# A hybrid encoder block with a product-key expert layer: more expert tiles ahead, and new places for a gelu, casts, copies and loads in the gate stage

## The chip, the cores and the metric

The kernel runs on one core of one Trainium2 chip, as one program. Its time is the device time of an execution, in microseconds (us). The time before is the median of 3 runs, and one more execution was profiled: the page and the trace belong to that one. Engine names are those of the profile: PE is TensorE's matmuls and PEld its weight loads, DVE is VectorE, ACT is ScalarE, POOL is GpSimd, and SP is the queue that issues most transfers.

## The reference, cut to what matters

512 tokens of 1024 float32 values pass a mixing layer and then an expert layer (PEER). The mixing layer (a gated group and a banded attention group, about the first 225 us of the kernel) is not touched by the change. The expert layer is:

```python
def block(xb):                                   # 128 tokens at a time
    q = (xb @ w_query).reshape(128, 8, 2, 128)   # 8 heads
    sc = einsum('thpd,hpkd->thpk', q, sub_keys)  # two score lists of 128 keys
    s_top, i_top = lax.top_k(sc, 16)
    cand = s_top[:, :, 0, :, None] + s_top[:, :, 1, None, :]
    best, pos = lax.top_k(cand, 16)              # 16 experts of 16384 for each head
    g = softmax(best)
    h = gelu(einsum('thkd,td->thk', take(expert_u, eidx), xb))
    return einsum('thk,thkd->td', g * h, take(expert_v, eidx))
```

So each token meets 8 x 16 of 16384 experts, each with a row of 1024 values in `expert_u` and one in `expert_v`.

## The kernel before, in words

**Dense and gathered tokens.** The first 128 tokens have their expert rows gathered by indirect DMAs. The other 384 are computed densely, against all 16384 experts: a first product of the expert rows with the tokens (gelu of it is `act`), then `act` times a gate that is zero for experts not chosen, then a second product with the rows of `expert_v`. The last 64 of them are mixed: their first products are gathered (64 gathers of 128 rows, L655, with the dots on VectorE at L665), and only their second product is dense. Dense first products therefore have 320 tokens.

**Split operands.** Each float32 operand of a large matmul is split in two halves: ScalarE copies the upper part (`hi`, L155) and another engine subtracts to get the rest (`lo`, L156). That engine is VectorE or GpSimd, as the caller asks. Three matmuls (`mm3`, L194 to L196) make one k-step, and eight k-steps one tile of 128 experts. Two tiles are a chunk; there are 64 chunks. The tokens' own halves lie in `xbh`, `xbl`; from the gate stage on in `xch`, `xcl`, which GpSimd copies (L912, L913) in the loop over routed heads, both at head 4.

**Stages.** After the mixing layer, a loop over 8 heads (L884) does the queries, the scores, the top-16 searches on VectorE and some first products between them. The gate stage (L1011) builds the dense gate: for 8 tokens at a time GpSimd multiplies two digit patterns into `bm` (L964), VectorE builds a one-hot `am` (L972), and TensorE multiplies them (16 matmuls, L980); ScalarE copies the result out and stores it to DRAM. Its iterations run n = 0 to 49; `bm` of n is built in iteration n and multiplied in n + 2. The order of TensorE, VectorE, ScalarE and GpSimd is written out by hand there (`manual_schedule`), iteration by iteration: `bm`, products of n - 2, gelu of finished first products, `am`, one dot, one gather on GpSimd, then a share of first products (`multiply_some`, with `some` k-steps), then at most one split of a next tile (`split_next`). The splits that GpSimd takes here are all of those with n up to 5 and then every third tile.

**Early gate weights.** For the 64 mixed tokens, `weights_early` (L676) runs in two parts: at n = `own` - 7 = 33 a copy on VectorE and a DMA issued by GpSimd (L681, L682), at n = 35 a gelu on ScalarE in place and a product with the gates on VectorE (L684, L685). At n = 37 the gates of these tokens are transposed on TensorE (L942, L943).

**The second-product loop.** For chunks 0 to 63, `second_product` (L1143) multiplies `act` by the gate (L1153), splits it (L1154, L1155), and multiplies with rows of `expert_v` (36 matmuls of 512 columns, L1187); then first products of chunk c + AHEAD follow (`ahead`), as long as there are any. AHEAD is 23, so 46 tiles are made before the loop. Only TensorE's order is written out; the other engines' order comes from a planner with priorities, bounded by `queued_behind` and `issue_after`, which put instructions behind a named one on the same engine. Every third chunk from 0 routes one head of the gathered tokens (`route_gathered`, L1091: scores loaded, top-16 searches, `pairs` with two casts on ScalarE at L760 and L761, `choose`, softmax), and the gathers with their dots (L1111, L1113) and weighted sums (L1122, L1124) are spread over the chunks. Before the loop GpSimd's queue issues, in this order, the second part of the first gates (L997), two rows of tokens (L1087, L1089), and the scores of the first routed head (L1095).

## Time and profile before

| | us |
|---|---|
| median of 3 runs | 1427.35 (1424.94 to 1428.87) |
| the profiled execution | 1427.15 |
| its span, first to last instruction | 1425.1 |
| TensorE busy in it | 1390.5 |
| VectorE busy | 1152.2 |
| GpSimd busy | 705.3 |
| ScalarE busy | 614.3 |

In the profile, a row of a timeline gives the start, the length, the engine, the line of the code, the instruction with the tiles it writes and reads, how many are merged in the row, and in brackets the time the engine stood idle before it and what ended that. A row of the waits gives the engine and line that waited, what it waited for, the sum, the count and the longest. A row of busy times gives a stretch, its length, busy time and count for each of PE, PEld, DVE, ACT and POOL, then TensorE's granted clock (1.00 is full), the DMA engines' share and GB/s. Matmuls overlap, so a matmul's length in the trace is longer than the time from its start to the next one's; the text goes by starts.

### The profile page before, as it was taken

Reading aid. Unit: us, or ns where it says so; the run is one execution under the profiler, and the core shown is the slowest. Engines: PE = TensorE matmul, PEld = TensorE weight load, DVE = VectorE, ACT = ScalarE, POOL = GpSimd, SP = SyncE. Lnnn points to the kernel's source line nnn. Section 1 sums busy time; section 2 is a strip of 40 time slices with the busy share of each in tenths; the row PEclk is TensorE's granted clock in tenths of the full one; section 3 lists DMA queues with packets and bytes.
Section 4 is the critical chain, followed back from the end, with each engine's and each line's share of the span. In section 5 each row is a group of like instructions: output and inputs, shape, how many; then the busy total and the mean of one; then the engine's idle time right before and its main releaser. Section 6 shows DMA issues by size and latency. Waiting matters only on the chain.

```text
span 1425.1 us, 21665 instructions
## 1 busy us (share of the span) xinstructions
PE 1390.5 (98%) x7838; PEld 1229.4 (86%) x7838; DVE 1152.2 (81%) x2502; ACT 614.3 (43%) x957; POOL 705.3 (49%) x487
## 2 busy tenths in 40 slices
PE   9999999999998988999999999999999999999998
PEld 7887788898998887888998998998998988888887
DVE  5537745898997888699999999888978888688883
ACT  5447635443443444455444444343433333333331
POOL 0002104678789997344545656556545454254620
PEclk9999999999999999999999999999999999999999
DMA  4452225668677997968998999999999999689991
GB/s 164 132 192 74 104 75 192 208 223 278 226 246 245 331 339 221 334 239 318 341 349 335 361 340 368 338 376 372 379 334 358 350 341 376 236 328 350 343 335 70
DMA packets 164331, 396.24 MB, mean 278 GB/s; under 512 B 12881, under 2 KB 75233, under 8 KB 162177
## 3 DMA queue, kind: packets, MB, share of 16 engines
q1 hardware_dynamic: 64640, 194.14, 37.9%
q0 software_dynamic: 48176, 173.46, 33.2%
q10 hardware_dynamic: 51408, 27.27, 6.5%
q8 instruction: 61, 1.00, 0.3%
q14 instruction: 46, 0.37, 0.1%
HBM read 363.34 MB, written 31.46 MB: 277 GB/s over the span
## 4 chain that ended last, share of the span: by engine, by line
PE 56%; DVE 0%; issue 0%
PE pa L1187 24%; PE px L1187 12%; PE pu L194 7%; PE pu L195 7%; PE pu L196 7%; DVE res L1225 0%
## 5 line engine op out<-in xcount | busy, mean ns | idle before, releaser
L155 ACT ACTIVATE hi<-raw 128x1024 fp32r<-128x1024 f32 x296 | 313.0, 1059 | 477.2 <-DMA raw<-in_vd 129.0
L156 DVE TENSOR_TENSOR lo<-raw,hi 128x1024 fp32r<-128x1024 f32 x241 | 296.0, 1229 | 81.9 <-ACT hi L155 80.9
L1111 POOL DMA_INDIRECT row<-in_ud,eint x128 | 199.8, 1561 | 185.6 <-DVE acc L1124 129.3
L1122 POOL DMA_INDIRECT row<-in_vd,eint x128 | 184.2, 1439 | 173.1 <-DVE row L1113 118.8
L194 PE MATMUL pu<-xch,hi 128*128 128x320 f32 x784 | 248.3, 317 | 4.4 <-ACT act L718 4.4
L195 PE MATMUL pu<-xcl,hi 128*128 128x320 f32 x784 | 243.6, 311 | 0.0
L196 PE MATMUL pu<-xch,lo 128*128 128x320 f32 x784 | 243.5, 311 | 0.0
L1187 PE MATMUL pa<-lo,wh 128*128 128x512 f32 x512 | 199.8, 390 | 0.0
L1187 PE MATMUL pa<-hi,wh 128*128 128x512 f32 x512 | 199.3, 389 | 0.0
L156 POOL TENSOR_TENSOR lo<-raw,hi 128x1024 fp32r<-128x1024 f32 x55 | 131.2, 2400 | 117.6 <-ACT hi L155 116.8
L1124 DVE SCALAR_TENSOR_TENSOR acc<-row,hw,acc 128x1024 f32<-128x1024 f32 x128 | 164.6, 1286 | 2.0 <-DMA row<-in_vd,eint 1.8
L1187 PE MATMUL pa<-hi,wl 128*128 128x512 f32 x512 | 158.5, 389 | 0.0
L1113 DVE SCALAR_TENSOR_TENSOR row<-row,xb 128x1024 f32<-128x1024 f32 x128 | 157.2, 1231 | 0.1
L194 PEld LDWEIGHTS pu<-xch,hi 128*128 128x128 f32 x784 | 148.8, 190 | 6.6 <-ACT act L718 4.9
L195 PEld LDWEIGHTS pu<-xcl,hi 128*128 128x128 f32 x784 | 148.8, 190 | 1.6
L196 PEld LDWEIGHTS pu<-xch,lo 128*128 128x128 f32 x784 | 148.5, 189 | 0.0
L980 PE MATMUL pa<-bm,am 128*128 128x128 f32 x768 | 98.6, 283 | 16.8 <-POOL bm L964 16.2
L1187 PEld LDWEIGHTS pa<-hi,wh 128*128 128x128 f32 x512 | 96.1, 188 | 20.6
L1187 PEld LDWEIGHTS pa<-hi,wl 128*128 128x128 f32 x512 | 96.1, 188 | 20.3
L1187 PEld LDWEIGHTS pa<-lo,wh 128*128 128x128 f32 x512 | 96.1, 188 | 20.2
L980 PEld LDWEIGHTS pa<-bm,am 128*128 128x128 f32 x768 | 94.0, 198 | 20.5 <-POOL bm L964 19.3
L1187 PE MATMUL px<-hi,wh 128*128 128x512 f32 x256 | 100.2, 391 | 1.6 <-ACT hi L155 1.6
(236 smaller groups left out, 2635.5 us busy)
## 6 DMA issues: line engine op xcount, KB each, us to landing
raw<-in_uT SPq DMA_DIRECT2D x128, 512.0 KB
raw<-in_vd SPq DMA_DIRECT2D x128, 512.0 KB
gd<-gst ACTq DMA_DIRECT2D x24, 1024.0 KB
gc<-gd SPq DMA_DIRECT2D x15, 1280.0 KB
raw<-in_w_in SPq DMA_DIRECT2D x19, 512.0 KB
raw<-in_wq SPq DMA_DIRECT2D x16, 512.0 KB
raw<-in_w_out SPq DMA_DIRECT2D x8, 512.0 KB
gc<-gd SPq DMA_DIRECT2D x15, 256.0 KB
```

The costliest lines, as they stand in the source:

```text
L155: top = nc.scalar.activation(hi, raw, AF.Copy)
L156: ins = eng.tensor_tensor(lo, raw, hi.bitcast(F32), op=ALU.subtract)
L194: nc.tensor.matmul(ps, lh[0], rh[0], start=first, stop=False)
L195: nc.tensor.matmul(ps, lh[0], rh[1], start=False, stop=False)
L196: nc.tensor.matmul(ps, lh[1], rh[0], start=False, stop=last)
L980: nc.tensor.matmul(ps[:, i * P:(i + 1) * P], am[:, 4 * q + i, :], bm[:, 4 * q + i, :], start=True, stop=True)
L1111: nc.gpsimd.indirect_dma_start(out=row, out_offset=None, in_=ud, in_offset=bass.IndirectOffsetOnAxis(ap=eint[:, j:j + 1], axis=0))
L1113: nc.vector.scalar_tensor_tensor(row, row, 1.0, xb0, op0=ALU.mult, op1=ALU.mult, accum_out=hw[:, j:j + 1])
L1122: nc.gpsimd.indirect_dma_start(out=row, out_offset=None, in_=vd, in_offset=bass.IndirectOffsetOnAxis(ap=eint[:, j:j + 1], axis=0))
L1124: nc.vector.scalar_tensor_tensor(acc0, row, hw[:, j:j + 1], acc0, op0=ALU.mult, op1=ALU.add)
L1187: nc.tensor.matmul(accs[t][half], (wh, wh, wl)[k][:, b, tok], w[b][k % 2][:, ds_], start=first and k == 0, stop=last and k == 2)
```

## The change

Seven edits:

- AHEAD goes from 23 to 25: 50 tiles instead of 46 are made before the second-product loop, with two more `act` buffers; the scratch of GpSimd's DMA descriptors is halved (`SCRATCH`).
- In the gate stage a split goes to GpSimd only for every fourth tile, and from the first iterations on.
- `weights_early` has three parts: the copy at n = 33, the DMA at n = 34, gelu and product at n = 36. The gelu's result goes to PSUM, and the product reads it there.
- The casts of a routed head are queued behind the gelu last recorded (head 0) or the casts of the head before (later heads).
- The copies to `xch`, `xcl` are made in four pieces, one each at heads 1 to 4.
- The scores of routed head 0 are loaded first on GpSimd's queue, and the gates' second part and the two rows behind them.
- The gate products of chunk 0 are queued behind the last `am` of the gate stage.

```diff
-AHEAD = 23
+AHEAD = 25
...
-SCRATCH = 4096
+SCRATCH = 2048
...
             if part == 0:
                 nc.vector.tensor_copy(dots[own, :, 0, :], d[own])
+            elif part == 1:
                 nc.gpsimd.dma_start(dots[own, :, 1, :], d[0:P - UX])
             else:
-                nc.scalar.activation(dots[own], dots[own], AF.Gelu_apprx_tanh)
-                nc.vector.tensor_tensor(gate[own, TT - 1, :], gate[own, TT - 1, :],
-                                        dots[own].rearrange("p a b k -> p (a b k)"), op=ALU.mult)
+                ps = pa()[own, 0:NH * TOPK]
+                nc.scalar.activation(ps, dots[own].rearrange("p a b k -> p (a b k)"), AF.Gelu_apprx_tanh)
+                nc.vector.tensor_tensor(gate[own, TT - 1, :], gate[own, TT - 1, :], ps, op=ALU.mult)
...
-                nc.scalar.activation(first[:, 1], pos[:, :, 0, :], AF.Copy, scale=float(NK))
-                nc.scalar.copy(top[:, 1, :, 1, :], pos[:, :, 1, :])
+                with queued_behind(behind):
+                    casts = (nc.scalar.activation(first[:, 1], pos[:, :, 0, :], AF.Copy, scale=float(NK)),
+                             nc.scalar.copy(top[:, 1, :, 1, :], pos[:, :, 1, :]))
+                    routed[:] = [getattr(i, "ins", i) for i in casts]
...
-            if h == 4:
+            if 1 <= h < 5:
 
                 with queued_behind(splits):
-                    nc.gpsimd.tensor_copy(xch, xbh[:, :, T0:T0 + NDU])
-                    nc.gpsimd.tensor_copy(xcl, xbl[:, :, T0:T0 + NDU])
+                    ks = slice((h - 1) % 2 * KT // 2, ((h - 1) % 2 + 1) * KT // 2)
+                    to, of = ((xch, xbh), (xcl, xbl))[(h - 1) // 2]
+                    nc.gpsimd.tensor_copy(to[:, ks, :], of[:, ks, T0:T0 + NDU])
...
+            marked[:] = [getattr(ins, "ins", ins)]
...
-                if n == own - 5:
+                if n == own - 6:
                     weights_early(1)
+                if n == own - 4:
+                    weights_early(2)
...
-                    split_next(nc.vector if split % 3 and n > 5 else nc.gpsimd)
+                    split_next(nc.vector if split % 4 else nc.gpsimd)
...
+        def scores_of(b, eng):
             n = NH // PARTS
             sc = ep.tile([P, n, 2, NK], F32, name="sc0", tag="sc0", bufs=2)
-            (nc.sync if b else nc.gpsimd).dma_start(sc.rearrange("p h a n -> p h (a n)"), s0d[b * n:(b + 1) * n].rearrange("h p a -> p h a"))
+            load = eng.dma_start(sc.rearrange("p h a n -> p h (a n)"),
+                                 s0d[b * n:(b + 1) * n].rearrange("h p a -> p h a"))
+            return sc, getattr(load, "ins", load)
+
+        xb0 = ep.tile([P, D], F32, name="xb0")
+        acc0 = ep.tile([P, D], F32, name="acc0")
+        scores = {0: scores_of(0, nc.gpsimd)}
+        with tc.issue_after(scores[0][1]):
+            load_gates(0, nc.gpsimd, range(1, len(GROUPS)))
+            nc.gpsimd.dma_start(xb0, xbd[0])
+            nc.gpsimd.dma_start(acc0, x2d[0])
...
-            choose(ep, pairs(ep, top, pos, n), n, best, to, mask,
+            choose(ep, pairs(ep, top, pos, n, behind=list(routed if b else done)), n, best, to, mask,
```

More of the change, by code (lines that the diff above doesn't have):

```diff
@@ L681, in weights_early @@
                 nc.vector.tensor_copy(dots[own, :, 0, :], d[own])
+            elif part == 1:
                 nc.gpsimd.dma_start(dots[own, :, 1, :], d[0:P - UX])
             else:
-                nc.scalar.activation(dots[own], dots[own], AF.Gelu_apprx_tanh)
-                nc.vector.tensor_tensor(gate[own, TT - 1, :], gate[own, TT - 1, :],
-                                        dots[own].rearrange("p a b k -> p (a b k)"), op=ALU.mult)
-        begun, more, done, behind = [], [], [], []
+                ps = pa()[own, 0:NH * TOPK]
+                nc.scalar.activation(ps, dots[own].rearrange("p a b k -> p (a b k)"), AF.Gelu_apprx_tanh)
+                nc.vector.tensor_tensor(gate[own, TT - 1, :], gate[own, TT - 1, :], ps, op=ALU.mult)
+        begun, more, done, behind, routed = [], [], [], [], []
         open_tile = []
@@ L747, in best_keys, with pairs @@
             return top16(top[:, 0, u, p2, :], pos[:, u, p2, :], src, rep)
-        def pairs(pool, top, pos, n, ps=None, own=False):
+        def pairs(pool, top, pos, n, ps=None, own=False, behind=()):
             if ps is None:
@@ L971, in first_one_hot @@
             am = gp.tile(full, F32, name="am", tag="am", bufs=LEAD + 1)
-            nc.vector.tensor_tensor(am, iota_k[:, None, :].to_broadcast(full),
-                                    g[:, 0, c * TC:(c + 1) * TC, None].to_broadcast(full), op=ALU.is_equal)
+            ins = nc.vector.tensor_tensor(am, iota_k[:, None, :].to_broadcast(full),
+                                          g[:, 0, c * TC:(c + 1) * TC, None].to_broadcast(full), op=ALU.is_equal)
+            marked[:] = [getattr(ins, "ins", ins)]
             return am
@@ L988, in store @@
                                 st.rearrange("p (q b) t -> p q (b t)", b=GB))
-        gcs = {}
+        gcs, marked = {}, []
         def load_gates(q, eng, parts=range(len(GROUPS))):
@@ L1083, in hybrid_block @@
         gcp.append(ep)
-        load_gates(0, nc.gpsimd, range(1, len(GROUPS)))
+        def scores_of(b, eng):
+            n = NH // PARTS
+            sc = ep.tile([P, n, 2, NK], F32, name="sc0", tag="sc0", bufs=2)
+            load = eng.dma_start(sc.rearrange("p h a n -> p h (a n)"),
+                                 s0d[b * n:(b + 1) * n].rearrange("h p a -> p h a"))
+            return sc, getattr(load, "ins", load)
         xb0 = ep.tile([P, D], F32, name="xb0")
-        nc.gpsimd.dma_start(xb0, xbd[0])
         acc0 = ep.tile([P, D], F32, name="acc0")
-        nc.gpsimd.dma_start(acc0, x2d[0])
+        scores = {0: scores_of(0, nc.gpsimd)}
[3 more added lines that the diff above has]
+            nc.gpsimd.dma_start(acc0, x2d[0])
         def route_gathered(b):
             n = NH // PARTS
-            sc = ep.tile([P, n, 2, NK], F32, name="sc0", tag="sc0", bufs=2)
-            (nc.sync if b else nc.gpsimd).dma_start(sc.rearrange("p h a n -> p h (a n)"), s0d[b * n:(b + 1) * n].rearrange("h p a -> p h a"))
+            sc = (scores.pop(b) if b in scores else scores_of(b, nc.sync))[0]
             top, pos = keys(ep, n)
@@ L1140, in hybrid_block @@
         accs = [[acx[:, 0:512], acx[:, 512:]]] + [[pa() for _ in range(2)] for _ in range(ND - 1)]
-        marked, own_last = [], []
+        own_last = []
         def second_product(c, between):
```

## The prediction

> **What bounds the kernel now.** I read the page's engine shares first, then the busy time by stretch, then TensorE's own waits, and only then the timelines of the stretches in which TensorE stood still.
>
> ```profile
> span 1425.1 us, 21665 instructions
> PE 1390.5 (98%) x7838; PEld 1229.4 (86%) x7838; DVE 1152.2 (81%) x2502; ACT 614.3 (43%) x957; POOL 705.3 (49%) x487
> ```
>
> ```profile
> 436.77:540.99 104.22, 92.06 (x721) 89.28 (x720) 89.09 (x147) 48.72 (x82) 99.12 (x63) 0.97 0.96 308
> 540.99:583.84 42.85, 36.67 (x291) 35.51 (x290) 31.67 (x39) 20.16 (x36) 31.23 (x17) 0.96 0.79 225
> 583.84:620.00 36.16, 30.17 (x171) 28.29 (x170) 26.94 (x100) 15.75 (x26) 4.93 (x7) 0.91 0.76 263
> 620.00:850.00 230.00, 230.00 (x1262) 207.60 (x1262) 219.92 (x508) 107.17 (x156) 122.77 (x83) 1.00 0.91 338
> 620.00:1419.00 799.00, 799.00 (x4192) 708.07 (x4192) 688.78 (x1118) 316.90 (x450) 391.25 (x262) 1.00 0.89 333
> ```
>
> Columns of the second fence: stretch and length, busy time of PE, PEld, DVE, ACT and POOL, granted clock, DMA share, GB/s. TensorE is the bound: 98% overall, and busy without a break from 620 to 1419. The change takes no matmul away, so it can only win back time that TensorE loses, and almost all of that lies in three stretches: A (436.77 to 540.99) and B (540.99 to 583.84), the gate stage, and C (583.84 to 620), the passage into the second product. In A GpSimd is busy 99.12 of 104.22.
>
> ```profile
> PE pa L980 <- POOL bm L964: 16.2, 11, 2.5
> PE pu L194 <- ACT act L718: 4.4, 2, 3.4
> PE px L1187 <- ACT hi L155: 1.6, 1, 1.6
> PE pa L196 <- POOL lo L156: 1.5, 1, 1.5
> PE pa L943 <- DVE gate L685: 1.5, 1, 1.5
> ```
>
> So TensorE waits for GpSimd's one-hot product bm (16.2 us), for a gelu (4.4), and three times for about 1.5.
>
> **The price of the matmuls.** From TensorE's timeline (start, length, instruction, idle time before it):
>
> ```profile
> 474.38 1.95 PE L980 MATMUL pa<-bm,am 128*128 128x128 f32 x16
> ...
> 477.05 1.95 PE L980 MATMUL pa<-bm,am 128*128 128x128 f32 x16
> ...
> 480.16 1.95 PE L980 MATMUL pa<-bm,am 128*128 128x128 f32 x16
> ...
> 538.76 1.95 PE L980 MATMUL pa<-bm,am 128*128 128x128 f32 x16
> ...
> 540.99 1.95 PE L980 MATMUL pa<-bm,am 128*128 128x128 f32 x16
> ```
>
> An iteration with two k-steps of a first product takes 477.05 - 474.38 = 2.67, one with one k-step 540.99 - 538.76 = 2.23, so a k-step (three matmuls) costs 0.44 and an expert tile (eight) 3.5. The set of four transposes adds 3.11 - 2.67 = 0.44. The loop hands out ceil(left / (50 - n)) k-steps. With AHEAD 23, left starts at 80 (the loop is to bring the count of finished tiles from 32 to (23 - 2) x 2 = 42, eight k-steps each): two per iteration to n = 29, one after. With 25 it starts at 112 (to 46): three to n = 12 (two at n = 2), then two to the end. A holds iterations 2 to 34: TensorE's work in it is 28 x 2.67 + 5 x 2.23 + 0.88 = 86.8, so 104.2 - 86.8 = 17.4 are lost. B holds 35 to 49: 15 x 2.23 + 0.44 = 33.9, lost 8.9.
>
> **AHEAD 25 and the split rule, stretch A.** 32 k-steps (14.1 us) leave the second-product loop: two before A (0.9), 15 in A (6.6), 15 in B (6.6). They are free only as far as TensorE waits there anyway. A becomes 23 x 2.67 + 10 x 3.11 + 0.88 = 93.4 of work. How long A lasts is GpSimd's affair:
>
> ```profile
> L156 POOL TENSOR_TENSOR lo<-raw,hi x5: 2373/2384/2390, 441.6 to 503.6; 128x1024 fp32r<-128x1024 f32 x5
> L156 DVE TENSOR_TENSOR lo<-raw,hi x4: 1217/1672/2469, 478.3 to 528.4; 128x1024 fp32r<-128x1024 f32 x4
> ```
>
> ```profile
> 464.95 0.98 POOL L655 DMA_INDIRECT rowe<-in_ud,eui  x1 [0.16 <-issue]
> ...
> 490.57 1.79 POOL L655 DMA_INDIRECT rowe<-in_ud,eui  x1 [0.16 <-issue]
> ```
>
> Five splits run on GpSimd in A now (2.38 each). Working the loop through with the new rule, tiles 36 and 40 stay on GpSimd in A (n = 5, 18) and nine go to VectorE (n = 2, 3, 4, 8, 11, 14, 22, 26, 30) where four do now. So GpSimd sheds 3 x 2.38 = 7.1. But a VectorE split isn't free for it: the gather at 490.57 ran beside one and took 1.79 instead of 0.98. At 0.8 each, five more cost 4.0. Net -3.1: A would last 101.1. VectorE, 89.09 busy now, gains 5 x 1.22 to 5 x 2.47, so it stands at 95 to 101 of 101; two engines that wait on each other, both near full, lose something, and I put 1 us: A = 102. Then 8.6 stay lost in A instead of 17.4, and the 0.9 ahead of A is absorbed too: gain 17.4 - 8.6 + 0.9 = **9.7**. Ends: no loss left, 17.4; and each of the five added splits, at the 2.47 end, holding GpSimd 1.25 longer too: A 101.1 + 6.2 = 107.3, gain 4.4.
>
> [...]
>
> **The early gate weights, stretch B.**
>
> ```profile
> 542.96 0.78 POOL L682 DMA_DIRECT2D dots<-du  x1 [2.82 <-PE pa L980]
> ...
> 545.63 2.39 POOL L156 TENSOR_TENSOR lo<-raw,hi 128x1024 fp32r<-128x1024 f32 x1
> 547.94 5.71 POOL L964 TENSOR_TENSOR bm<-hb,lb 128x1024 f32<-128x1024 f32 x3
> ```
>
> ```profile
> 546.49 7.32 DVE L685 TENSOR_TENSOR gate<-gate,dots 64x128 f32<-64x128 f32 x1 [0.37 <-ACT dots L684]
> ...
> 553.84 1.22 DVE L972 TENSOR_TENSOR am<-iota_k,pa 128x1024 f32<-128x1024 f32 x1
> ...
> 555.29 0.29 DVE L956 TENSOR_TENSOR hb<-hb,pa 128x128 f32<-128x128 f32 x1
> ```
>
> Two accidents lose B's 8.9. GpSimd idles 2.82 before the DMA at L682, which waits for the last dots on VectorE while the next bm is queued behind it; one iteration later the dots are done and that bm is ahead of it. And the 64x128 product at L685 lasts 7.32: it ends when GpSimd's back-to-back run ends (547.94 + 5.71 = 553.65), and am and the transposes wait. With the gelu written to PSUM the product has one PSUM operand, like the 0.29 at L956; I take 0.3. The price of the move: the DMA now sits behind bm of n = 34 and ahead of tile 44's split, so bm of n = 35 ends 1.9 + 0.78 + 2.39 + 1.9 = 7.0 after bm of n = 33 against two iterations of TensorE, 5.3: 1.7 lost. Gelu and transposes stand only one iteration apart now; that costs nothing as long as the 16 KB DMA lands within two iterations, else up to 3. B = 15 x 2.67 + 0.44 + 1.7 = 42.2 with 6.6 more work in it: gain 8.9 - 1.7 = **7.2**, ends 4 and 8.9.
>
> **The casts behind the gelu, scores ahead, stretch C.**
>
> ```profile
> 592.34 0.58 POOL L997 DMA_DIRECT2D gc<-gd  x1 [13.27 <-DMA gd<-gst]
> ```
>
> ```profile
> 602.79 0.22 ACT L760 ACTIVATE top<-pos 128x16 f32<-128x16 uint32 x1 [6.38 <-DVE pos L738]
> ...
> 606.20 0.49 ACT L1167 ACTIVATE wh<-gc 128x128 fp32r<-128x128 f32 x2
> 606.60 0.41 ACT L718 ACTIVATE act<-pu 128x320 f32<-128x320 f32 x1
> ```
>
> ```profile
> 607.07 0.64 PE L194 MATMUL pu<-xch,hi 128*128 128x320 f32 x1 [3.38 <-ACT act L718]
> 607.50 0.47 PE L195 MATMUL pu<-xcl,hi 128*128 128x320 f32 x1
> ...
> 612.57 0.47 PE L196 MATMUL pu<-xch,lo 128*128 128x320 f32 x1
> ...
> 616.36 0.41 PE L194 MATMUL pu<-xch,hi 128*128 128x320 f32 x1 [1.04 <-ACT act L718]
> ```
>
> ScalarE stood 6.38 in front of a cast whose positions VectorE hadn't found, with the gelu that frees TensorE's PSUM tile queued behind it; TensorE then idled 3.38 and ran slow: (612.57 - 607.50) / 19 = 0.267 a matmul against 0.44 / 3 = 0.147, for the 5.5 us from 607.07 to 612.57, of which 2.5, and the last one's 0.1, are lost: 2.6. Queued behind the gelu of that chunk, the casts can't do this; behind them wait the adds of that head's pairs on VectorE and its first gathers, which TensorE doesn't wait for. Scores loaded first no longer stand behind the 13.27 us wait at L997, so VectorE can start that head while it has nothing else; the second part of the gates is now queued behind them on GpSimd, and feeds only the last tokens of chunk 0 (L1167), 14 us after its issue at 592.34: covered, unless the scores' own tile comes free later than that wait ends. I count 3.38 + 2.6 = **6.0**, and leave the 1.04 (a gelu that came late on ScalarE) and the 1.6 at px where they are. Ends: 0 (the wait returns at the next chunk) and 8.6.
>
> [...]
>
> **The operand's copies, in the heads.**
>
> ```profile
> 308.62 2.32 POOL L912 CAST xch<-xbh 128x2560 fp32r<-128x2560 f32 x1
> 310.89 2.32 POOL L913 CAST xcl<-xbl 128x2560 fp32r<-128x2560 f32 x1
> ```
>
> ```profile
> 324.13 0.50 PE L196 MATMUL pa<-xbh,lo 128*128 128x512 f32 x1 [1.55 <-POOL lo L156]
> ```
>
> 4.6 us of copies stand in one head ahead of gathers and splits, and TensorE waits 1.55 for a split there. In four pieces of about 1.2 the wait should go: **1.5**, ends 0 and 1.5.
>
> **At nothing:** chunk 0's products with the gates, queued behind the last am on VectorE (their gates, loaded by GpSimd late in the same stage, come after it anyway, and behind them stand only splits that TensorE reaches in C); two more act tiles; gathers paced over 93 steps instead of 95 (2% denser); the halved descriptor scratch, whose only trace is "issue" time, bounded by one 0.16 gap for each of some 24 gathers in A, 4 us.
>
> **The sum.** 9.7 + 7.2 + 6.0 + 1.5 = 24.4. The profiled execution took 1427.15 (span 1425.1 and 2.05 around it), 0.2 under the median of 1427.35; 1427.15 - 24.4 = **1402.8**.
>
> **The rivals.**
> *VectorE takes over and the passage gives back.* For it: VectorE is 219.92 of 230 busy from 620 to 850, and densest where the routed heads start, so C's 6.0 could come back as a late lo split; A may not shorten at all. Against: TensorE never waits there now. Price: A 4.4, B 4, C and copies 0: 8.4 gained, 1418.8. Chance 0.17, with 0.08 more in which the second-product loop loses a further 4 to 12 us and nothing measurable is left, 1423 to 1431.
> *Slower: the splits lock the two engines.* A VectorE split caught behind a GpSimd run without a pause is the 7.32 row again, 6.1 over its own 1.22. In A the gathers leave a pause of 0.16 nearly every iteration; in B they have ended and three splits (n = 38, 42, 46) fall there. All twelve caught: 12 x 6.1 = 73 lost, 24.4 gained, about 1476. It decides from (24.4 + 4.3) / 12 = 2.4 us of delay a split. Against: the four in A now took at most 2.47 in all. Chance 0.05.
> [...]
> *It doesn't do what it says.* The planner, not the diff, orders ScalarE and VectorE after the gate stage; the scores' tile may lie over a gate tile and load no earlier. Then C gives 0: 1402.8 + 6.0 = 1408.8. Chance 0.1, inside the range.
>
> **How the numbers follow.** The forecast has 0.60. All losses gone would give 17.4 + 8.9 + 8.6 + 1.5 = 36.4, 1390.8; the first rival stands at 1418.8. Range 1392 to 1419. A measurement of this kernel tells about 0.3%, 4.3 us, from no change: faster 0.60 + 0.17 + 0.1 = 0.87, same 0.08, slower 0.05.
>
> **What would show it.** TensorE's wait for bm falls from 16.2 to about 8; L685 drops from 7.32 to about 0.3; the 2.82 before L682 and the 3.38 at L194 are gone; TensorE is unbroken from about 610 (620 now: 2.2 less in A, 0.7 in B, 6.0 in C, 1.5 in the heads) and the loop has two fewer chunks with first products; VectorE splits in the gate stage show 1.2 to 2.5. I am wrong if TensorE shows new waits after the passage, if waits for am or lo take the place of those for bm, or if VectorE's splits exceed 2.5.

## The result, and the profile after

The changed kernel takes 1420.21 us (median of 6 runs, 1416.75 to 1421.07) beside 1428.11 (6 runs, 1424.85 to 1432.68) for the kernel before: ratio 0.9948, 95% interval 0.9930 to 0.9965. The gain is 7.9 us; the forecast was 24.4 and its range ended at 1419. The profiled execution took 1418.47. The page and TensorE's waits of the changed kernel (in its numbering L985 is the gate products, L968 `bm`, L976 `am`, L719 the gelu, L762 and L763 the casts, L803 and L804 the softmax's subtraction and its exp, L1202 the second product):

```profile
span 1416.7 us, 21660 instructions
PE 1387.3 (98%) x7838; PEld 1224.6 (86%) x7838; DVE 1157.5 (82%) x2505; ACT 610.5 (43%) x955; POOL 699.0 (49%) x486
```

```profile
PE pu L194 <- ACT act L719: 9.7, 6, 4.7
PE pa L985 <- DVE am L976: 5.0, 2, 4.7
PE pa L985 <- POOL bm L968: 2.8, 8, 1.1
PE px L1202 <- DVE wl L1170: 1.6, 1, 1.6
```

The wait for `bm` did fall, from 16.2 to 2.8. Two waits that the prediction had named as signs of its failure stand in its place: 5.0 for `am` in the gate stage and 9.7 for the gelu, all but about 1 us of that from the passage on. To see where time was won and given back, put marks on the same matmuls in both traces (starts on TensorE's timeline, us; "set" is one of the gate stage's 48 sets of 16 products, "chunk" the first matmul of a chunk's second product):

| mark | before | after | gain since the mark above |
|---|---|---|---|
| set 0 (stretch A begins) | 436.77 | 438.10 | -1.3 |
| set 33 (B begins) | 540.99 | 542.09 | +0.2 |
| chunk 0 | 590.30 | 590.92 | +0.5 |
| chunk 3 (behind the passage) | 653.21 | 652.14 | +1.7 |
| chunk 9 | 744.81 | 743.74 | 0 |
| chunk 18 | 882.21 | 885.90 | -4.8 |
| chunk 39 | 1202.81 | 1206.50 | 0 |
| chunk 42 (two chunks of first products fewer) | 1241.57 | 1231.04 | +14.2 |
| last matmul | 1420.86 | 1412.39 | -2.1 |

The 14.2 of the loop are the 32 k-steps that moved ahead of it. Up to chunk 0 only 0.6 were paid for them, so the stage gained 13.6. Of that, set 0 to set 33 holds 0.2 + 6.6 (15 of the moved k-steps) = 6.8, and set 33 to chunk 0 holds 0.5 + 6.6 = 7.1; ahead of set 0, 0.88 of the 1.3 are the two k-steps there, and 0.4 is lost. The passage (chunk 0 to chunk 3) gained 1.7, and the loop lost 4.8 and 2.1. The sum, 8.4, is the difference of the two spans.

The same stretches of the gate stage, then chunks 9 to 18, by windows of the changed kernel (columns as in the prediction's windows):

```profile
438.10:542.09 103.99, 97.52 (x766) 94.97 (x765) 100.65 (x150) 52.37 (x87) 96.19 (x59) 0.98 0.99 320
542.09:584.48 42.39, 40.96 (x337) 40.46 (x336) 27.05 (x41) 22.63 (x39) 29.62 (x18) 1.00 0.86 252
```

```profile
743.74:885.90 142.16, 138.32 (x759) 123.91 (x757) 135.59 (x264) 62.33 (x91) 77.67 (x54) 1.00 0.93 346
```

A has not become shorter, it holds more work: VectorE has gone from 89.09 to 100.65 busy there, GpSimd from 99.12 to 96.19. Now the three places where the gain was cut. **Gate stage**, rows of the changed kernel's timeline:

```profile
445.21 3.69 DVE L156 TENSOR_TENSOR lo<-raw,hi 128x1024 fp32r<-128x1024 f32 x1
...
451.68 2.38 POOL L156 TENSOR_TENSOR lo<-raw,hi 128x1024 fp32r<-128x1024 f32 x1
454.02 1.91 POOL L968 TENSOR_TENSOR bm<-hb,lb 128x1024 f32<-128x1024 f32 x1
456.09 1.79 POOL L655 DMA_INDIRECT rowe<-in_ud,eui  x1 [0.16 <-issue]
...
451.95 5.07 DVE L156 TENSOR_TENSOR lo<-raw,hi 128x1024 fp32r<-128x1024 f32 x1
456.94 1.21 DVE L976 TENSOR_TENSOR am<-iota_k,pa 128x1024 f32<-128x1024 f32 x1
...
458.29 3.59 PE L985 MATMUL pa<-bm,am 128*128 128x128 f32 x16 [4.74 <-DVE am L976]
```

VectorE's split began 0.27 behind GpSimd's own split. It ended at 457.02, about 1.1 after GpSimd's split and the `bm` that followed it without a pause (454.02 + 1.91 = 455.93), so by its end it stood still for both and then ran about its usual length (1.22, the median of VectorE's splits over the whole execution). `am` is queued behind it and TensorE waits 4.74.

**Passage**, ScalarE and TensorE of the changed kernel:

```profile
613.42 0.21 ACT L762 ACTIVATE top<-pos 128x16 f32<-128x16 uint32 x1
...
613.61 0.22 ACT L762 ACTIVATE top<-pos 128x16 f32<-128x16 uint32 x1
...
616.46 0.19 ACT L763 CAST top<-pos 128x16 f32<-128x16 uint32 x1
...
621.52 0.22 ACT L804 ACTIVATE ex<-ex 128x16 f32<-128x16 f32 x1
...
627.81 0.21 ACT L804 ACTIVATE ex<-ex 128x16 f32<-128x16 f32 x1 [3.15 <-DVE ex L803]
627.93 1.99 ACT L155 ACTIVATE hi<-raw 128x1024 fp32r<-128x1024 f32 x2
629.94 1.28 ACT L719 ACT_TABLE_LOAD   x1
631.23 0.77 ACT L719 ACTIVATE act<-pu 128x320 f32<-128x320 f32 x2
...
631.72 0.41 PE L194 MATMUL pu<-xch,hi 128*128 128x320 f32 x1 [4.71 <-ACT act L719]
```

```profile
632.00:640.00 8.00, 8.00 (x38) 7.45 (x38) 2.86 (x8) 0.00 (x0) 2.26 (x3) 0.79 1.00 409
```

The first cast now comes behind a gelu, at 613.42, and TensorE passes where it stood 3.38 before. The second routed head's casts are queued behind the first's, and start at 613.61. The exps at 621.52 and 627.81 are, by their order, those of the first and the second head. ScalarE stands 3.15 in front of the second one, whose input VectorE has not made; two `hi`, a table load and the gelu follow, and TensorE waits 4.71 and then runs at 0.79 of its clock for 8 us (1.7 more). **Loop:** the same picture in chunks 9 to 18, ahead of one of three late gelus (0.78, 0.92 and 2.13 of TensorE's time at 753, 800 and 848):

```profile
797.10 0.22 ACT L804 ACTIVATE ex<-ex 128x16 f32<-128x16 f32 x1 [4.19 <-DVE ex L803]
```

### The profile page after: what moved, and what is told of

Its sections match the earlier page's. It is cut to its first block, busy times and chain, and to the rows that moved or that the text cites. A ratio compares the mean times of both kernels' runs of the same rounds, so it can differ in the third digit from the quotient of the medians.

```text
span 1416.7 us, 21660 instructions
## 1 busy us (share of the span) xinstructions
PE 1387.3 (98%) x7838; PEld 1224.6 (86%) x7838; DVE 1157.5 (82%) x2505; ACT 610.5 (43%) x955; POOL 699.0 (49%) x486
## 4 chain that ended last, share of the span: by engine, by line
PE 31%; DVE 12%; DMA 8%; issue 4%; ACT 1%; POOL 0%; SPq 0%; DVEq 0%; ACTq 0%; POOLq 0%
PE pa L1202 13%; PE px L1202 6%; PE pu L194 4%; PE pu L196 4%; PE pu L195 4%; DMA gc<-gd 4%; DVE lo L156 3%; DVE row L1128 2%; DVE acc L1139 2%; DMA row<-in_ud,eint 2%; DVE act L1168 1%; DMA raw<-in_uT 1%; DMA row<-in_vd,eint 1%; DVE wl L1170 1%; DMA raw<-in_vd 1%
## 5 line engine op out<-in xcount | busy, mean ns | idle before, releaser
L156 DVE TENSOR_TENSOR lo<-raw,hi 128x1024 fp32r<-128x1024 f32 x244 | 307.0, 1259 | 72.1 <-ACT hi L155 71.6
L1137 POOL DMA_INDIRECT row<-in_vd,eint x128 | 179.7, 1404 | 192.0 <-DVE row L1128 131.5
L1202 PE MATMUL pa<-lo,wh 128*128 128x512 f32 x512 | 199.7, 390 | 0.0
L1202 PE MATMUL pa<-hi,wh 128*128 128x512 f32 x512 | 199.4, 389 | 0.0
L156 POOL TENSOR_TENSOR lo<-raw,hi 128x1024 fp32r<-128x1024 f32 x52 | 124.1, 2401 | 116.3 <-ACT hi L155 115.3
L1202 PE MATMUL pa<-hi,wl 128*128 128x512 f32 x512 | 158.4, 389 | 0.0
L1202 PEld LDWEIGHTS pa<-hi,wh 128*128 128x128 f32 x512 | 96.1, 188 | 20.6
L1202 PEld LDWEIGHTS pa<-hi,wl 128*128 128x128 f32 x512 | 96.1, 188 | 20.2
L1202 PEld LDWEIGHTS pa<-lo,wh 128*128 128x128 f32 x512 | 96.1, 188 | 20.2
L985 PE MATMUL pa<-bm,am 128*128 128x128 f32 x768 | 96.3, 279 | 7.9 <-DVE am L976 5.0
L985 PEld LDWEIGHTS pa<-bm,am 128*128 128x128 f32 x768 | 92.3, 194 | 10.8 <-issue 5.5
L1202 PE MATMUL px<-hi,wh 128*128 128x512 f32 x256 | 100.1, 391 | 0.6 <-ACT hi L155 0.6
```

Of the source, the lines that this page charges most:

```text
L156: ins = eng.tensor_tensor(lo, raw, hi.bitcast(F32), op=ALU.subtract)
L985: nc.tensor.matmul(ps[:, i * P:(i + 1) * P], am[:, 4 * q + i, :], bm[:, 4 * q + i, :], start=True, stop=True)
L1137: nc.gpsimd.indirect_dma_start(out=row, out_offset=None, in_=vd, in_offset=bass.IndirectOffsetOnAxis(ap=eint[:, j:j + 1], axis=0))
L1202: nc.tensor.matmul(accs[t][half], (wh, wh, wl)[k][:, b, tok], w[b][k % 2][:, ds_], start=first and k == 0, stop=last and k == 2)
```

## The experiments

All changes are against the changed kernel unless it says otherwise. The ratio is to the kernel before, run on the same chip; 0.001 is 1.4 us. The last three columns are from the profiles: set 0 to set 47, chunk 0 to chunk 3, chunk 9 to chunk 18, in us. Two small edits of the change have no run of their own: the gate products of chunk 0 queued behind the last `am`, and the halved scratch, which is in only_ahead together with AHEAD.

| kernel | ratio, 95% interval | gate stage | passage | chunks 9-18 |
|---|---|---|---|---|
| before | 1 | 144.9 | 62.9 | 137.4 |
| changed | 0.9948, 0.9930 to 0.9965 | 143.7 | 61.2 | 142.2 |
| only_ahead | 1.0049, 1.0029 to 1.0069 | 160.5 | 60.9 | 138.7 |
| ahead23 | 0.9974, 0.9961 to 0.9987 | 139.5 | 62.2 | 140.1 |
| old_splits | 0.9996, 0.9981 to 1.0012 | 152.3 | 62.1 | 142.3 |
| weights_old | 0.9975, 0.9956 to 0.9994 | 147.7 | 61.4 | 141.8 |
| splits_vector | 1.0015, 1.0000 to 1.0031 | 148.8 | 62.0 | 142.2 |
| copies_old | 0.9949, 0.9931 to 0.9968 | 144.0 | 61.9 | 142.2 |
| exp_behind | 1.0155, 1.0131 to 1.0178 | 143.8 | 58.4 | 143.5 |
| casts_free | 0.9908, 0.9883 to 0.9934 | 143.8 | 55.9 | 141.0 |
| scores_old | 0.9950, 0.9929 to 0.9970 | 143.8 | 61.3 | 144.9 |
| scores_only (on before) | 0.9967, 0.9951 to 0.9983 | 148.6 | 57.1 | 137.6 |
| gathers_late | 0.9916, 0.9897 to 0.9935 | 143.7 | 60.8 | 137.4 |
| route_late | 0.9969, 0.9947 to 0.9991 | 144.6 | 56.8 | 143.6 |
| route2_late | 0.9908, 0.9884 to 0.9932 | 144.4 | 58.4 | 142.7 |
| free_late | 0.9875, 0.9852 to 0.9898 | 143.7 | 55.9 | 137.4 |
| free_mod2 | 0.9949, 0.9932 to 0.9966 | 149.9 | 55.6 | 141.1 |
| free_late_mod2 | 0.9912, 0.9886 to 0.9937 | 150.2 | 56.3 | 137.4 |
| free_pace | 0.9848, 0.9818 to 0.9877 | 143.7 | 56.2 | 137.4 |
| free_late_n5 | 0.9866, 0.9837 to 0.9896 | 145.0 | 56.0 | 137.4 |

### What made room in the gate stage

**only_ahead**, the kernel before with two lines of the change:

```diff
-AHEAD = 23
+AHEAD = 25
-SCRATCH = 4096
+SCRATCH = 2048
```

> The kernel before with AHEAD 25 alone (and the smaller descriptor scratch that makes room for it). Theory (the stage's waits take the added k-steps whoever splits the tiles): the stage grows by no more than 4 us, 1414 to 1419 us, so that all else in the change together is worth nothing or less. Rival (the split rule and the move of the gate weights are needed, since GpSimd is at 99 of 104 us in the stage and every added tile's split falls to it): the stage grows by 7 to 14 us and the time is 1421 to 1429 us.

1435.49 us, slower than before, and beyond both. The stage grew by 15.7, more than the 13 us of work added between its marks. One of VectorE's splits lasted 7.77 us (the median is 1.93), and TensorE's waits for `am` alone came to 10.6:

```profile
L156 DVE TENSOR_TENSOR lo<-raw,hi x11: 1215/1929/7771, 466.2 to 609.5; 128x1024 fp32r<-128x1024 f32 x11
```

**ahead23**:

```diff
-AHEAD = 25
+AHEAD = 23
```

> The changed kernel with AHEAD 23 as before, all else kept. Theory (the gate stage's length is set by GpSimd and VectorE taking turns, and the 32 k-steps moved into it, 14.1 us, ride in TensorE's waits): the stage stays within 4 us of its length and the 14.1 us come back in the loop, 1430 to 1434 us. Rival (the new split rule and the gelu to PSUM shorten the stage by themselves, and the first products fill only part): the stage is 7 us or more shorter and the time is 1421 to 1426 us.

1424.33 us, in the rival's range, but the stage is only 4.2 shorter than with 25, though it holds 13 us less work: just outside the theory's 4 and short of the rival's 7. So the other edits shorten the stage by 5.3 without added work, and added work alone lengthens it by 15.7; together they cost nothing. The gain belongs to the pair.

**old_splits**, and **weights_old**, in which the gate weights' DMA goes with the copy at n = 33 again and the gelu at n = 35:

```diff
-split_next(nc.vector if split % 4 else nc.gpsimd)
+split_next(nc.vector if split % 3 and n > 5 else nc.gpsimd)
```


```diff
-elif part == 1:
...
-ps = pa()[own, 0:NH * TOPK]
-nc.scalar.activation(ps, dots[own]..., AF.Gelu_apprx_tanh)
-nc.vector.tensor_tensor(gate[own, TT - 1, :], gate[own, TT - 1, :], ps, op=ALU.mult)
+nc.scalar.activation(dots[own], dots[own], AF.Gelu_apprx_tanh)
+nc.vector.tensor_tensor(gate[own, TT - 1, :], gate[own, TT - 1, :], dots[own]..., op=ALU.mult)
...
-if n == own - 6:
+if n == own - 5:
     weights_early(1)
-if n == own - 4:
-    weights_early(2)
```

> The changed kernel with the old split rule in the gate stage (VectorE from n = 6 on and two of three, GpSimd at n = 2, 3, 4). Theory (in the stage GpSimd is what is full, so the room for the 14.1 us of added first products comes of the splits that leave it, as the prediction has it): the stage from the first product to the fiftieth grows by 5 to 10 us against the changed kernel's 143.7 (to its 47th iteration), 1425 to 1430 us. Rival (VectorE's splits lock GpSimd's runs as long as they save it, as the 5.07 us one does): the stage stays within 3 us, 1418 to 1423 us.

> The changed kernel with the early gate weights as before: the DMA and the gelu in one part at n = 44, the gelu written in place, so that the product on VectorE reads two SBUF operands. Theory (the 7.32 us product and the 2.82 us of GpSimd standing before the DMA come back, worth 7 us in the prediction): the product lasts 5 us or more again and the stage grows by 4 to 8 us, 1424 to 1428 us. Rival (with more splits on VectorE the run of GpSimd behind which the product stood is broken up, so the move is worth little): the stage stays within 2 us, 1419 to 1422 us.

1429.12 and 1423.73 us, with the stage 8.6 and 4.0 us longer. Both first theories hold (the second time is 0.3 below its range): the split rule is worth 6.8 us by the ratios, the move of the weights 3.9. The product at L685 lasts 6.90 when both its operands lie in SBUF again (7.32 before), and 0.29 in the changed kernel, with one of them in PSUM (two rows, one of each kernel):

```profile
546.51 6.90 DVE L685 TENSOR_TENSOR gate<-gate,dots 64x128 f32<-64x128 f32 x1 [1.02 <-ACT dots L684]
```

```profile
548.23 0.29 DVE L687 TENSOR_TENSOR gate<-gate,pa 64x128 f32<-64x128 f32 x1
```

**splits_vector**:

```diff
-split_next(nc.vector if split % 4 else nc.gpsimd)
+split_next(nc.vector)
```

> The changed kernel with every split of the gate stage's tiles on VectorE, none on GpSimd. Theory (the 5.07 us split that costs TensorE 4.7 us at 458 stood still behind GpSimd's own split and the one-hot product right after it; with no split on GpSimd no such run forms): no split on VectorE lasts over 3.7 us in the stage, the wait of 4.7 for am is gone, and the stage is 2 to 5 us shorter (143.7 to its 47th iteration), 1415 to 1419 us. Rival (VectorE is then the full engine, or its splits stand behind one-hot products and gathers as long): waits for am of 3 us or more stay and the stage is no shorter, 1420 to 1426 us.

1427.79 us: the rival, and 1.8 above its range. The stage is 5.1 longer than the changed kernel's, and TensorE's waits for `am` come to 9.5. The meeting moved, and became longer. From its timeline:

```profile
544.87 5.89 DVE L156 TENSOR_TENSOR lo<-raw,hi 128x1024 fp32r<-128x1024 f32 x1
...
543.95 5.73 POOL L968 TENSOR_TENSOR bm<-hb,lb 128x1024 f32<-128x1024 f32 x3
```

Three `bm` in one run, from 543.95 to 549.68; the split that began inside it ended at 550.76. Three more kernels tried other arrangements, on top of two edits that are told below (free casts in all three, `DELAY = 14` in the last two): **free_mod2** and **free_late_mod2** with the first line, **free_late_n5** with the second.

```diff
-split_next(nc.vector if split % 4 else nc.gpsimd)
+split_next(nc.vector if split % 4 != 2 else nc.gpsimd)
...
+split_next(nc.vector if split % 4 and n > 5 else nc.gpsimd)
```

> The changed kernel with free casts, and in the gate stage GpSimd's one split in four moved by two tiles (rest 2 instead of 0). Theory (the 4.7 us wait for am at 458 is one meeting: a VectorE split that starts as GpSimd's own split and a one-hot product run without a pause; it hangs on which tile GpSimd takes): the longest VectorE split before 470 us falls below 3.7, that wait is under 2 us, 1407 to 1410 us. Rival (the meeting happens wherever GpSimd has a split, as 5.9 us at 545 with none on GpSimd suggests): a split of 5 us or more is found elsewhere in the stage, and the time is within 2 us of free casts alone, 1411 to 1416 us.

> The changed kernel with free casts, DELAY 14 and GpSimd's splits moved by two tiles. If the three losses (passage, loop, the one meeting in the gate stage) are independent: 1401 to 1406 us, about what the prediction gave for the change itself. If the third is only moved: 1405 to 1410 us.

> The changed kernel with free casts and DELAY 14, and with the splits of the gate stage up to n = 5 on GpSimd, as before the change; from n = 6 on one in four. With free casts and DELAY 14 alone the stage took 143.8 us from its first product to the 47th iteration, with a split of 5.1 us on VectorE at 452 and a wait of 4.7 for am behind it. Theory (each meeting with a run of GpSimd has its price, and the early splits on VectorE fall among the densest of GpSimd's work): that wait goes and the stage takes 140 to 143 us, 1405 to 1409 us. Rival (GpSimd is the full engine and falls behind by what it takes over, or the meeting happens at a later tile): 146 us or more, 1412 to 1418 us.

1421.08, 1414.58 and 1410.52 us. The first two are rivals, and both times lie about 5 us above the rivals' ranges: the wait of 4.7 at 458 went, but with a split of 5.89 us elsewhere and waits for `am` of 11.5 and 11.6 us in all (5.0 in the changed kernel) the stage is 6 us longer. In the third the wait of 4.7 went, as its theory says, and waits for `bm` (5.3 instead of 2.7) came in its place: the stage stands at 145.0, between the two bounds, and its ratio is the same as free_late's. In scores_only, whose edit touches no line of this stage, the stage is 3.7 longer than before, with a single wait of 3.28 for `am` at 533.6. So the same stage can fall into a meeting in one profile and miss it in another, and a comparison with the one profile of the kernel before is uncertain by as much. No arrangement tried was without a meeting; whether one exists is open.

**copies_old**, both whole copies in the fifth head:

```diff
-if 1 <= h < 5:
-    ...
-    nc.gpsimd.tensor_copy(to[:, ks, :], of[:, ks, T0:T0 + NDU])
+if h == 4:
+    nc.gpsimd.tensor_copy(xch, xbh[:, :, T0:T0 + NDU])
+    nc.gpsimd.tensor_copy(xcl, xbl[:, :, T0:T0 + NDU])
```

> The changed kernel with the operand's two whole copies in the fifth head again, as before. The prediction counted 1.5 us for the four pieces. If that is what they give: the wait for lo at about 324 us returns with 1.5 us and the time is 1421.5 to 1422.5 us. Rival (the pieces move the waits to other heads, where the first gate product comes as late as before): the first product of the gate stage starts within 0.5 us of the changed kernel's 438.1, and the time is within 1 us of it.

1421.88 us beside a ratio equal to the changed kernel's. The wait for `lo` is back at 325 (2.98), set 0 of its profile starts at 441.81, and the times do not show it. In the kernels that differ from the changed one only behind set 0, it starts anywhere between 436.1 and 440.4; 441.81 is 1.4 above that, but one profile cannot price this edit.

### What took the passage's gain back

**exp_behind**: the casts of every head, and the softmax's exp, behind the last gelu issued:

```diff
-pairs(ep, top, pos, n, behind=list(routed if b else done))
+pairs(ep, top, pos, n, behind=list(done))
...
-nc.scalar.activation(ex, ex, AF.Exp)
+with queued_behind(behind):          # softmax(ep, best, n, behind=list(done))
+    nc.scalar.activation(ex, ex, AF.Exp)
```

> The changed kernel, with the casts of every routed head and also the exp of its softmax queued on ScalarE behind the gelus issued so far. Theory 1 (the head that starts in the passage gives its gain back through ScalarE's queue: the casts no longer stand in front of a gelu, the exp of the same head does): the 4.7 us wait of TensorE for the gelu at 631.7 goes, with the slow clock behind it, and the 0.9 at 800: 6 to 8 us faster than the changed kernel, 1412 to 1415 us, and chunk 3 of the second product starts about 6 us earlier. Rival (VectorE's work is what is late, and whatever ScalarE runs first the gelu or the split of one of the next tiles comes late): chunk 3 starts no more than 2 us earlier, 1418 to 1421 us, and waits for hi or lo or raw take the place of the wait for the gelu.

1448.64 us, far above both ranges. My first theory was that the exp is the next thing to be queued. It failed: the wait for the gelu in the passage shrank only from 4.71 to 3.45, and from chunk 15 to chunk 36 the kernel lost 28.3 us against the changed one. New rows of its waits:

```profile
PE pu L194 <- ACT act L719: 11.5, 10, 3.5
PE px L1203 <- DVE lo L156: 7.7, 8, 2.4
...
PE pu L196 <- DVE lo L156: 4.8, 9, 2.0
```

The exp waits for a gelu and so for TensorE, VectorE's sum waits for the exp, and the splits behind that sum on VectorE come late. That chain is read from the order of the queues; the rows show only that the splits came late, as the rival has it, and the run moved the later heads' casts together with the exp, so the two are not told apart.

**casts_free**, **scores_old** (the scores loaded last again), and **scores_only** (the new load order alone, on the kernel before: the second diff the other way round):

```diff
-pairs(ep, top, pos, n, behind=list(routed if b else done))
+pairs(ep, top, pos, n, behind=())
```


```diff
-scores = {0: scores_of(0, nc.gpsimd)}
-with tc.issue_after(scores[0][1]):
-    load_gates(0, nc.gpsimd, range(1, len(GROUPS)))
-    ...
+load_gates(0, nc.gpsimd, range(1, len(GROUPS)))
+...
+scores = {0: scores_of(0, nc.gpsimd)}
```

> The changed kernel with the two casts of each routed head free of the gelus again, as before the change; scores and all else stay. Theory (the passage is held by VectorE's load, the casts are one of several things that ScalarE can be caught in front of): the wait in the passage changes its place, chunk 3 of the second product starts 61 to 64 us after chunk 0 (61.2 with the casts queued), 1418 to 1423 us. Rival (the prediction's step: casts in front of the gelu cost 6 us): chunk 3 starts 66 us or more after chunk 0, 1424 to 1428 us.

> The changed kernel with the scores of the first routed head loaded last again, behind the gates' second part and the two rows. Theory (the earlier load lets the first head start in the passage, where VectorE has no room, so it only moves the loss): chunk 3 starts within 2 us of the changed kernel's distance from chunk 0 (61.2), and the time is within 3 us of it. Rival (the prediction: the scores ahead are what makes the passage shorter): chunk 3 comes 3 us or more later, 1424 to 1427 us.

> The kernel before with one part of the change: the scores of the first routed head loaded ahead of the gates' second part and the two rows; the casts stay free, AHEAD 23, all else as before. In the changed kernel with free casts chunk 0 to chunk 3 took 55.9 us, with queued casts 61.2, with queued casts and the old load order 61.3, in the kernel before 62.9. Theory (the scores ahead alone give the passage's whole gain and the queue takes it back): chunk 0 to chunk 3 takes 55 to 57 us, and the time is 1419 to 1424 us (6 us less than before, of which the loop may take 3). Rival (free casts and scores ahead need the filled gate stage, since the chunks that are ahead leave TensorE something to do): 60 us or more, 1425 to 1429 us.

1412.32, 1419.99 and 1424.34 us. Both expectations for casts_free were wrong: freeing the casts gains 5 to 6 us. The first theories of the other two hold, scores_only's to within 0.4 us. From chunk 0 to chunk 3 the four combinations are as follows; the kernel before and scores_only have the old gate stage, the other three the new one:

| | casts free | casts queued |
|---|---|---|
| scores last | 62.9 (before) | 61.3 (scores_old) |
| scores ahead | 55.9 (casts_free), 57.1 (scores_only) | 61.2 (changed) |

Three pairs differ in one edit. With free casts the scores ahead are worth 5.8 (before and scores_only), about all that the prediction counted for the passage; the queue takes 5.3 back (casts_free and the changed kernel); and with the casts queued the scores ahead are worth 0.1 (scores_old and the changed kernel). The other kernels agree: 55.6 to 57.1 in all seven with the scores ahead and free casts, 60.8 to 62.2 in the seven with the scores ahead, the casts queued, and exps and heads left where they were. Only with the scores late may the queue gain, 1.6, and that pair differs in the gate stage too. ScalarE and TensorE of casts_free:

```profile
598.52 0.22 ACT L762 ACTIVATE top<-pos 128x16 f32<-128x16 uint32 x1 [3.19 <-DVE pos L739]
...
600.86 0.21 ACT L762 ACTIVATE top<-pos 128x16 f32<-128x16 uint32 x1 [1.49 <-DVE pos L739]
...
602.33 0.41 ACT L719 ACTIVATE act<-pu 128x320 f32<-128x320 f32 x1
602.76 1.28 ACT L804 ACT_TABLE_LOAD   x1
604.06 0.22 ACT L804 ACTIVATE ex<-ex 128x16 f32<-128x16 f32 x1
...
616.40 1.28 ACT L804 ACT_TABLE_LOAD   x1 [1.91 <-DVE ex L803]
617.70 0.21 ACT L804 ACTIVATE ex<-ex 128x16 f32<-128x16 f32 x1
...
602.80 0.41 PE L194 MATMUL pu<-xch,hi 128*128 128x320 f32 x1 [0.34 <-ACT act L719]
```

With its scores early, the first head needs no queue: VectorE has the positions at 598.52 instead of 602.79, the gelu is 0.34 late, and its exp is done at 604. The second head's exp, at 617.70, falls between two gelus, at 614.07 and 632.83, and TensorE does not wait there. With the queue the casts of both heads wait until 613.4, the exps come at 621.52 and 627.81, and the second one stands in front of a gelu that TensorE needs.

### What the loop gave back

**gathers_late** has the first edit alone (gathers of rows start eight steps later), **route_late** the first and the second (each routed head three chunks later), **route2_late** both and `ROUTE = 2` (heads at chunks 2, 4 and so on to 16):

```diff
-DELAY = 6
+DELAY = 14
```


```diff
-if c % ROUTE == 0 and c < PARTS * ROUTE:
-    route_gathered(c // ROUTE)
+if c % ROUTE == 0 and 0 < c <= PARTS * ROUTE:
+    route_gathered(c // ROUTE - 1)
```

> The changed kernel with DELAY 14 instead of 6: the rows gathered for the routed heads are paced from eight steps later. Theory (the loop's losses between chunks 9 and 39, some 4 us, come of VectorE being full in the first third of the second product, of which the routed heads are a part): with the heads' chosen rows due later, VectorE loosens there and 2 to 4 us come back, 1416 to 1418 us. Rival (the pacing touches GpSimd and the DMA queue alone, VectorE's order is unchanged): within 1.5 us of the changed kernel, or slower by up to 5 us because the gathers stand denser against the end.

> The changed kernel with DELAY 14 and every routed head three chunks later (the first at chunk 3), so that no routed head stands in the passage. Theory (what takes back the passage's gain is the work of the routed heads on VectorE: their searches stand between the lo splits there, the loads into the freed tiles come late, and ScalarE's hi and gelu behind them): the wait of 4.7 at 631 is gone, chunk 3 of the second product starts 4 to 6 us earlier than with DELAY 14 alone, and the time is 1409 to 1413 us. Rival (the wait at 631 comes of the exp's place in ScalarE's queue or of the gate weights of chunk 1, not of the load on VectorE): chunk 3 starts within 2 us of it and the time is 1414 to 1418 us.

> The changed kernel with the first routed head at chunk 2 and one at every second chunk after it, and DELAY 14. The late heads alone shortened chunk 0 to chunk 3 from 61.2 to 56.8 us and then lost 14 us between chunks 9 and 27, where heads and gathered rows stood together. Theory (VectorE cannot hold heads, gathered rows and splits at once; any pair of them fits): with the heads done by chunk 16 the loss between chunks 9 and 27 is under 5 us and most of the passage's 4 us stays: 1410 to 1415 us. Rival (the loss comes of the denser gathers alone, which DELAY 14 sets): 8 us or more are lost there again, 1419 to 1425 us.

1416.25, 1424.29 and 1414.91 us. Later gathers took the whole loss out of chunks 9 to 18, though 1.6 were lost again by chunk 27. Later heads gave the passage 4.0 us and lost 14.9 between chunks 9 and 27, where heads then overlapped with more gathers; heads in a quicker row lost 5.3 there and kept 2.4. By these arrangements the loss goes where heads and gathers meet.

**free_late** has free casts and `DELAY = 14`, **free_pace** free casts, `DELAY = 6` and this line, so that the gathers are spread over 95 steps again and not 93:

```diff
-weight = 2 * NCHK - AHEAD
+weight = 2 * NCHK - 23
```

> The changed kernel with free casts and DELAY 14, which took 8 and 5 us by themselves. Theory (they are two losses in two places, the passage and chunks 9 to 18): both come back, no loss between chunks 9 and 18 (137.4 us), 1405 to 1409 us. Rival (VectorE has a fixed load between 590 and 900 us, and what is freed at one place is lost at the next): 1410 to 1414 us, as with free casts alone.

> The changed kernel with free casts, DELAY 6 as it is, and the gathers paced over 95 steps again (weight of AHEAD 23), not 93. With free casts chunk 9 to chunk 18 took 141.0 us at AHEAD 25 (137.4 without any wait); with the scores ahead alone at AHEAD 23 it took 137.6. Theory (the 2 percent denser gathers are what makes the heads' searches come late there): 137.4 to 138.5 us, and 1408 to 1411 us. Rival (it is the order of the work after a fuller gate stage, and two percent are nothing): 140 us or more, 1411 to 1414 us.

1410.37 and 1407.63 us. The gains of the two edits add up: 0.0040 for the casts and 0.0032 for the delay against 0.0073 for both (each is uncertain by about 0.003). And with the casts free, two per cent in the gathers' pace are the whole loop loss; casts_free and free_pace differ in that line alone:

```profile
737.81:878.85 141.04, 138.06 (x759) 123.98 (x758) 133.62 (x232) 62.68 (x89) 80.20 (x54) 1.00 0.95 354
```

```profile
739.16:876.56 137.40, 137.40 (x758) 124.26 (x757) 130.84 (x222) 60.56 (x86) 73.79 (x54) 1.00 0.95 353
```

With the old pace TensorE is unbroken through chunks 9 to 18, and chunk 57 to chunk 63 also takes 48.96 instead of 50.92. It takes 48.96 in all four kernels with the old pace (before, ahead23, scores_only, free_pace) and more in every other one. The pace is not the only way to lose time in chunks 9 to 18: ahead23 has the old pace and queued casts, and lost 2.6 there, with two more late gelus (its waits from the passage on):

```profile
627.24 0.64 PE L194 MATMUL pu<-xch,hi 128*128 128x320 f32 x1 [4.77 <-ACT act L719]
...
778.42 0.41 PE L194 MATMUL pu<-xch,hi 128*128 128x320 f32 x1 [0.54 <-ACT act L719]
...
795.55 0.42 PE L194 MATMUL pu<-xch,hi 128*128 128x320 f32 x1 [1.62 <-ACT act L719]
```

So the new pace without the queue lost 3.6 (casts_free), the queue with the old pace 2.6 (ahead23), and both together 4.8 (the changed kernel). Free_pace is the fastest kernel here, 1.5% (1.2 to 1.8) under the kernel before and 1.0 point under the changed one. Its page:

```profile
span 1405.3 us, 21671 instructions
PE 1384.8 (99%) x7838; PEld 1224.2 (87%) x7838; DVE 1155.8 (82%) x2505; ACT 614.5 (44%) x957; POOL 698.0 (50%) x486
```

## Why the prediction was wrong, point by point

By the marks the gain is 8.4 of the 24.4. Of the 16 that are missing, the loop, put at nothing, has 6.9, the passage 4.3, the stretch ahead of set 0 2.8 (1.5 for the copies and 0.9 forecast, 0.4 lost), and A itself 2.0.

**The gate stage, A and B: mechanism right, A too large.** Forecast 9.7 + 7.2, found 6.8 + 7.1, one of the two parts to 0.1, by one profile each. The weights' move and the split rule each did what was said (weights_old, old_splits). A's shortfall has two pieces. That "the 0.9 ahead of A is absorbed too" is not borne out: set 0 starts 1.3 later, though its start varies by more than that from profile to profile. And VectorE's splits were priced at 1.2 to 2.5 from four rows of before; two of them took 3.69 and 5.07 now. The wait of 4.74 behind the second one, with the clock of 0.59 in the 4 us after it, cost 6.4 of the 10.6 that A still loses (103.99 - 93.4). "In A the gathers leave a pause of 0.16 nearly every iteration" is right, but there is one such pause in an iteration, and where GpSimd has a split of its own, that split and a `bm` run up to it without a break. The warning was a row of the same trace (7.32 at L685), which the prediction gave to a rival at 0.05 and kept out of A. That rival was wrong in size (it wanted all splits caught), right in kind.

**The lock between the two engines.** By its end, a VectorE split that began inside a run of GpSimd stood still until that run paused: 3.85 us through two instructions (5.07 - 1.22), 4.67 through a run of three (5.89 - 1.22). Both ended 1.1 behind the run (457.02 and 455.93; 550.76 and 549.68). With 1.9 us for a `bm` and 2.4 for a GpSimd split, both standstills are longer than any one instruction of their runs: in these rows the wait lasted about as long as what was left of the run (455.93 - 451.95 = 3.98, 549.68 - 544.87 = 4.81).

**The casts behind the gelu: the step that failed.** The prediction counted 6.0 for casts and scores together and said of the queue that "behind them wait the adds of that head's pairs on VectorE and its first gathers, which TensorE doesn't wait for". Found: 1.7, and by the two-by-two table the scores ahead alone give 5.8 while the queue costs 5.3. What waits behind the casts also includes the exps of the first two heads on ScalarE, the second of them in front of a gelu for which TensorE does wait. The stall was followed to VectorE and the gathers, not on to the end of the head's chain, which comes back to ScalarE. The prediction's own lower end, "0 (the wait returns at the next chunk)", is nearly what happened.

**The loop "at nothing": the other step that failed.** "gathers paced over 93 steps instead of 95 (2% denser)" was put at 0. With the casts free it measured 5.6 us by the marks (3.6 + 2.0), and 4.7 by the medians or 8.6 by the ratios (0.0060), which compare two chips; the last is uncertain by some 6. The prediction had the row that warns: VectorE 219.92 of 230.00 busy from 620 to 850. That VectorE at 96% had no room for 2% more, so that its lateness came out at an exp and then at a gelu, fits the wait of 4.19 at 797.10, but it is argued: no run loads VectorE alone.

**The copies in pieces:** 1.5 forecast; the wait for `lo` in the heads is gone, but set 0 came no earlier, and copies_old shows no difference in time by the ratio.

**The rivals.** "VectorE takes over and the passage gives back" (0.17, and 0.08 for a further loss in the loop) is nearest to what happened, but its 1418.8 is close to 1420.21 by luck: the gate stage gained more than its 8.4, and the loop lost 6.9, which only its addition has. The late `lo` split that it feared was a late gelu. "It doesn't do what it says" did not happen: the first search of head 0 starts 6.6 behind chunk 0 instead of 10.5. Most of the 24.4 were there to be had: free_pace, which is the change without the queue and with the old pace, gains 0.0152, 21.7 us.

## What to carry to other kernels

When work is queued behind an instruction to clear one wait, follow everything else of the same chain through the queue of every engine, up to the next instruction that the bounding engine needs: here casts moved by 13 to 15 us dragged an exp in front of a gelu. Where an engine that is not the bound is over nine tenths busy, as VectorE was here (219.92 of 230 us), don't take a change of its pace as free; test "at nothing" items on it one by one. And of a change in several parts, try each part left out: here one part left out and one side effect undone nearly tripled the gain.

## What the runs showed of the hardware

**VectorE behind a GpSimd run.** A subtraction with both inputs in SBUF, 1.22 us by its median in the changed kernel, took 5.07 (changed kernel, 451.95) and 5.89 us (splits_vector, 544.87) when it began inside a run of GpSimd without pauses. The 64x128 product of the gates took 6.90 with both inputs in SBUF (weights_old, 546.51; GpSimd's run ended at 553.26, the product at 553.41) and 0.29 with one input in PSUM (changed kernel, 548.23, inside GpSimd's run from 547.26).

**The clock after short waits.** In the kernel before, TensorE's clock in the 4 us behind a wait of 2.51 us fell to 0.67 (1.00 in the 4 us ahead of them), and behind one of 2.50 it stayed at 1.00:

```profile
451.30:455.30 4.00, 3.96 (x22) 3.81 (x22) 0.05 (x2) 1.17 (x2) 3.84 (x3) 0.67 1.10 349
...
507.90:511.90 4.00, 4.00 (x34) 4.00 (x34) 3.97 (x7) 1.32 (x3) 3.82 (x3) 1.00 0.89 302
```

So of two waits whose lengths differ by 0.01 us, one cost more than its time and the other did not. Behind the changed kernel's 4.74 at 458 the clock fell to 0.59 (1.00 from 449 to 453):

```profile
458.30:462.30 4.00, 4.00 (x20) 4.00 (x21) 3.97 (x8) 0.96 (x2) 2.51 (x2) 0.59 0.96 362
```
